# A rewritten order for ACT and DVE at the seam between the mixer and the feed-forward

## The chip, the cores and the metric

The kernel runs on one core of a Trainium2 chip. The metric is device time in microseconds (us), the median of several runs. PE is the matrix engine (TensorE), DVE the vector engine, ACT the scalar engine, POOL is GpSimd; SP issues most of the loads. A time inside the program is counted from the start of the profiled span.

## What is computed

One encoder layer on 512 rows of 1024 columns, in fp32:

```python
u = rms_norm(h, g_mix[i])
z = u @ w_in[i]
...                                     # two kinds of attention, each projected: y_a, y_b
mixed = gates[:, :, 0] * y_a + gates[:, :, 1] * y_b
h = h + mixed @ w_mix_out[i]            # the mixer's output
u = rms_norm(h, g_mlp[i])
h = h + jnp.square(jax.nn.relu(u @ w_ff1[i])) @ w_ff2[i]        # D_FF = 4096
ple_gate = jax.nn.sigmoid(rms_norm(h, g_ple[i]) @ w_ple_gate[i])
h = h + ple_gate * (p[i] @ w_ple_proj[i])
return rms_norm(h, g_final)
```

The change lies around the lines from the mixer's output to the feed-forward.

## The kernel before

**Split operands.** A product of fp32 matrices is made of three matmul passes over operands split in two: hi (a rounded copy) and lo (what is left), as hi·hi, hi·lo and lo·hi. The weights are split on the chip, in units of 128x1024 that are numbered in the order of use (u59h and u59l are the two parts of unit 59). ACT casts hi and DVE subtracts to get lo:

```python
nc.scalar.copy(hi[:, z], src[:, z])                                              # L329
nc.vector.tensor_tensor(lo[:, z], src[:, z], hi[:, z].bitcast(F32), ALU.subtract)  # L330
```

The hi and the lo parts have rings of four buffers each. `advance(i)` emits the splits up to unit i at the place in the program where it is called.

**Seven products for eight.** Blocks of 2x2 are multiplied by seven products, numbered 1, 2, 5, 6, 7, 3, 4 in the code. Products 5, 6, 7 and 4 take a weight that is a sum of quadrants, made in place in the loaded tile by `sum_source`: by a DVE add (L301) for the keys named there, else by a DMA from POOL's queue that adds into its target (L303). A sum for 6 may be made only when the unit of 5, whose tile it changes, is split.

**The feed-forward.** It runs in four quarters of 28 products each. A key ("f1", g, pn) is product pn with the first matrix for column group g, ("s2", g, pn) with the second. The list `steps` gives the order; quarter 1 in its short form, where a and b are ("f1", 0, .) and ("f1", 1, .), A and B ("s2", 0, .) and ("s2", 1, .):

```
a1 b1 a2 b2 a5 b5 a6 b6 a7 a3 b7 b3 A1 a4 b4 B1 A2 A5 B5 B2 A6 B6 A3 A7 B7 B3 A4 B4
```

These are units u59 to u86, so a1 is u59, a5 u63, a6 u65, A1 u71, B5 u77 and B6 u80; quarter 2 begins with u87. Before each product the loop over `steps` emits the evacuation of the one before (L925 copy, L929 add; into h_sb at L1122 and L1124), the activation (`ff1_act`: relu, square, cast; `ff1_lo`, L1430), the operands of the second matrix (`ff2_op`: L1415 to L1419, whose hi and lo are made at L72 and L73), the splits (`advance(last_unit(n + 2))`: two products ahead) and the weight sums.

**From the mixer to the quarter.** The mixer's last products end with h_sb = mxx + h_sb, and `part_ssq` (ACT, L1132) takes sums of squares of the rows. Each of the four row blocks then goes through: n_ms and n_rs on POOL (L364, L367: the factor of the norm), n_xn on DVE (L374), transposes n_tr on PE (L1192), and `put`, which writes hi (ACT, L1208) and lo (DVE, L1216) of the operands. For row blocks 2 and 3 the sums of operand quadrants s1 to s4 and their copies a21 are made on top of that (`t2_sums`, `t2_sums2`, `t2_sums34`, `t2_rest`). Independent of all that are eight products with w_ple_proj, pp 0 to 7 (L76 to L78, pspp, copied to ppo and spilled), which fill PE between the norms and transposes.

**What sets the order.** On PE and POOL it is always the order of the program. On ACT and DVE it is the order of the program from the mixer's output to step 3 of quarter 1 (`man.close()` at n == 3), and elsewhere a scheduler's. SP's order is the scheduler's. An engine takes its instructions strictly in order, so one that waits holds up all behind it.

Of the kernel before, what the change touches and what calls it, by code (L numbers as in the profile page):

```python
# [52 lines left out]
def layer_kernel(ctx: ExitStack, tc: tile.TileContext, x, p, g_mix, w_in, b_forget, swa_sinks,  # L53
# [32 lines left out]
    raws, order, unit_of = [], [], {}  # L86
# [77 lines left out]
    for t in MIX_STEPS.split():  # L164
# [3 lines left out]
        elif t[1:] in "04":  # L168
            half = int(t[1:]) // 4
# [9 lines left out]
            for j, u in enumerate(rows(w_ple_gate, r4 * 512, half * 512, f"wpg{half}{r4}")):  # L179
                add(("pg", half, 2 * r4 + j), u)  # L180

    look = {"split": 2, "dma": 4, "ahead": 3, "wp2": None, "n": 0, "d": 0}

    def raws_of(i):
        r, pn = order[i][1][:2]
# [95 lines left out]
    def sum_source(i):  # L281

        if i in sources or i >= len(order) or not isinstance(order[i][1][0], (list, dict)):
            return
        emit_dma(i)
        key, (rs, pn, _), _ = order[i]

        first = {5: 1, 6: 5, 4: 6}.get(pn)  # L290
        if (first and unit_of[key[:-1] + (first,)] >= look["n"]
                or pn == 7 and unit_of[key[:-1] + (5,)] not in sources
                or any(raws[r]["tile"] is None for r in raws_of(i))):
            return
        if pn in (1, 2, 3):
            q = quadrant(i, pn in (2, 3), pn == 3)
        else:
            q = quadrant(i, 0, pn == 7)
            other = quadrant(i, *{5: (0, 1), 7: (1, 1), 6: (1, 1), 4: (1, 0)}[pn])
            if key[0] == "s2" and pn in (5, 7) or key == ("f1", 1, 6):  # L300
                nc.vector.tensor_tensor(q, q, other, ALU.add)  # L301
            else:
                nc.gpsimd.dma_start(q, other, accum_op=ALU.add)  # L303
        sources[i] = q if key[0] != "f1" and key[0] != "g" else q.rearrange("q k (j c) -> q k j c", c=P)
# [28 lines left out]
    def advance(i):  # L333

        while look["n"] < min(len(order), i + 1):
            n = look["n"]
            emit_split(n)
            look["n"] += 1
            emit_dma(min(len(order) - 1, look["n"] + look["ahead"]))
            if isinstance(order[n][1][0], (list, dict)):  # L340

                key = order[n][0]
                for pn in {1: (5,), 5: (6, 7), 6: (4,)}.get(key[-1], ()):
                    if key[0] != "s2" or pn in (6, 4):
                        sum_source(unit_of[key[:-1] + (pn,)])

    def unit(key):
        i = unit_of[key]
# [834 lines left out]

    trs = {}

    def t2_pe(tb):
        for half in range(2):
            tr = trs[tb, half] = psA.tile([P, 4, P], F32, tag="tr", bufs=3,
                                          name=f"n2_{tb}_tr{half}")
            for j in range(4):  # L1190
                k = half * 4 + j
                nc.tensor.transpose(tr[:, j, :], xn2[tb][:, k * P:(k + 1) * P], ident)  # L1192
# [4 lines left out]
    def put(pn, tb, src, between=None):  # L1197
        sl = t2_cols(tb)
        k, parts = 0, []
        for hi, lo in zip(*u_op[pn]):  # L1200
            n = hi.shape[1]
            parts.append((hi[sl], lo[sl], src[:, k:k + n]))
            k += n
        for hi, lo, part in parts:
            if pn == 3:
                nc.scalar.mul(hi, part, -1.0)
            else:
                nc.scalar.copy(hi, part)  # L1208
# [22 lines left out]
        put(4, tb, trs[tb, 1],  # L1231
            lambda: nc.vector.tensor_tensor(s1, trs[tb, 1], a21, ALU.subtract))

    def t2_sums2(tb):
        a21, s1, s2, s3, s4 = sums[tb]
        nc.vector.scalar_tensor_tensor(s2, s1, -1.0, a_raw[0][t2_cols(tb)], ALU.mult,
                                       ALU.subtract)
        put(6, tb, s2)

    def t2_sums34(tb):  # L1240
        a21, s1, s2, s3, s4 = sums[tb]
        nc.vector.tensor_tensor(s3, a_raw[0][t2_cols(tb)], a21, ALU.subtract)
        nc.vector.tensor_tensor(s4, a_raw[1][t2_cols(tb)], s2, ALU.add)

    def t2_rest(pn):
        new_op(pn)
        for tb in (2, 3):
            put(pn, tb, sums[tb][{5: 1, 7: 3, 3: 4}[pn]])

    def scale2(tb):  # L1250
        rs = rms_rstd(acc2[tb], f"n2_{tb}")
        xn2[tb] = norm_scale(h_sb[:, tb, :], rs, gb, wk3, f"n2_{tb}")
# [56 lines left out]
    MIX_TAGS = {1: ("x", "sc"), 2: ("y", "tr"), 5: ("z", "mm"), 6: ("x", ""), 7: ("x", ""),  # L1309
                4: ("x", ""), 3: ("z", "")}  # L1310

    def mix_out(pn):
        for i in range(2):
            tb, half = rows_out("mx", MIX_TAGS, pn, i)
            if pn in (2, 3, 7, 4):
                part_ssq(acc2[tb], tb, half, "2")

    f1_0 = unit_of["f1", 0, 1]
# [2 lines left out]
    for t in MIX_STEPS.split():  # L1321
        if t == "B5":
            mix_ops(1, (3,))
            mxp.close()
            r_st.close()
            wk3 = ctx.enter_context(tc.tile_pool(name="wk3", bufs=2))
            look["place"] = ff_other
            p_sb = [tmp(f"p_sb{n}", (P, 2, 256)) for n in range(2)]
            for n in range(2):
                nc.sync.dma_start(p_sb[n], p[n * 256:n * 256 + 256, :]  # L1330
                                  .rearrange("(t q) c -> q t c", q=P))
            with nc.allow_non_contiguous_dma(reason="one word per partition and chunk"):
                nc.sync.dma_start(g_ple_t, g_ple[0].rearrange("(k q) -> q k", q=P))
        if done[:1] == "B":
            mix_out(int(done[1]))
        if t == "p4":
            break
        if t == "A5":
            mix_ops(1, (5,))
        if t == "B2":  # L1340
            mix_ops(1, (7, 6))
        if t == "B3":
            p_transposed()
        if t == "p0":
            scale2(0)
        key = ("mx", "AB".index(t[0]), int(t[1])) if t != "p0" else ("pp", 0)
        if t == "A4":
            scale2(1)
        if t == "B4":
            t2_pe(0)  # L1350
            new_u2()
            t2_top(0)
        advance(min(unit_of[key] + (4 if t in ("A1", "A2", "B1") else 3), f1_0))
        for n in range(look["n"], min(unit_of[key] + 5, f1_0)):
            sum_source(n)
        if t in ("A1", "A2"):
            mix_sum(1, 0 if t == "A1" else 2)
            mix_sum(1, 1 if t == "A1" else 3)
        if t == "p0":
            pp_put(0, pp_mm(0))  # L1360
        else:
            rows_mm("mx", t[0] == "A", MIX_TAGS, key, mix_op[key[1:]])
        done = t
# [84 lines left out]
    def last_unit(n):  # L1448
        return unit_of[steps[min(n, len(steps) - 1)]]


    look["split"] = 0
    t2_pe(1)
    ps = pp_mm(1)
    t2_top(1)
    scale2(2)
    scale2(3)
    pp_put(1, ps)
    pp_put(2, pp_mm(2))
    pp_put(3, pp_mm(3))  # L1460
    ps = pp_mm(4)
    t2_pe(2)
    t2_sums(2)
    pp_put(4, ps)
    advance(f1_0 + 1)
    t2_pe(3)
    t2_sums2(2)
    t2_sums(3)
    pp_put(5, pp_mm(5))
    advance(f1_0 + 2)  # L1470
    t2_sums2(3)
    pp_put(6, pp_mm(6))
    pp_put(7, pp_mm(7))
    advance(f1_0 + 3)
    t2_rest(5)
    done, late, later = None, None, {}
    for n, st_ in enumerate(steps):
        res = None
        if done is not None:
            if done[0] == "f1":  # L1480
                res = win_out(done[:2], done[2], tmp)
                if res is not None:
                    src, dst, i, e = res
                    res = src, dst, done[1], i, e
                if done[2] == 4:
                    for w, pn in ((1, 5), (1, 6), (5, 3), (6, 7)):
                        later.setdefault(n + w, []).append((done[1], pn))
            elif done[1] % 2:
                s2_out(done[1] // 2, done[2])
        if late is not None:  # L1490
            ff1_lo(*late)
        for g, pn in later.pop(n, ()):
            ff2_op(g, pn)
        if n > 0:
            advance(last_unit(n + 2))
            for i in range(look["n"], last_unit(n + 3) + 1):
                sum_source(i)
        if n in (3, 4):
            t2_sums34(n - 1)
        if n in (5, 6):  # L1500
            t2_rest({5: 7, 6: 3}[n])
        late = None if res is None else ff1_act(*res)
        if st_[0] == "f1":
            win_mm(st_[:2], st_[2], u_op[st_[2]], {})
        else:
            s2_mm(*st_[1:])
        if n == len(steps) - 2:
            t3(0)
        done = st_
        if n == 3:  # L1510
            man.close()
    s2_out(3, 4)
    t3(1)
# [112 lines left out]
```

## Time and profile before

| | |
|---|---|
| runs | 717.55, 717.98, 718.2 us |
| median | 717.98 us |
| profiled execution | 719.32 us |
| its span, first to last instruction | 717.6 us |
| granted TensorE clock | 0.997 |
| busy: PE, DVE, ACT, POOL | 702.9, 550.5, 456.6, 87.8 us |
| quarter 1, first matmul of u59 to that of u87 | 347.93 to 429.63: 81.70 us |
| quarter 2 | 429.63 to 506.04: 76.41 us |
| mean rate of the DMA | 168 GB/s |

The busy line gives each engine's share of the span. A window's row has the stretch, its length, and busy time with the number of instructions for each engine in it. A timeline row has start, duration, engine, line, operation, output and inputs without buffer numbers, and in brackets the idle time of the engine before it with what ended it. A row of PE's waits has the total, the number of times and the longest wait.

### The profile page before, as it was taken

To read this page: it belongs to the slowest core of one execution; us is meant where nothing else is said; L and a number is where in the kernel's file an instruction comes from. 1 tells how busy PE (TensorE), PEld (TensorE's weight loads), DVE (VectorE), ACT (ScalarE), POOL (GpSimd) and SP (SyncE) were. 2 spreads that over 40 slices of the span, in tenths; PEclk is the share of its full clock that TensorE was granted. 3 is DMA by queue.
4 is the path that set the end of the run, shared out by engine and by line. 5 is a ranking of instruction groups with operands and counts; after the bars stand their busy time and mean duration, and the time that the engine had idled before them with its cause. 6 is when DMAs were issued, how large, how long until landed. Compare 5 with 4: busy or idle time off the path is not lost.

```text
span 717.6 us, 11507 instructions
## 1 busy us (share of the span) xinstructions
PE 702.9 (98%) x4205; PEld 622.3 (87%) x4205; DVE 550.5 (77%) x941; ACT 456.6 (64%) x851; POOL 87.8 (12%) x129
## 2 busy tenths in 40 slices
PE   8999999999999999999999999999999999999996
PEld 7988888888888998888989779988998899988785
DVE  6557888877696766877799885899579965996565
ACT  5547888779862564347688536874487547865452
POOL 1011211100001200203020102010200020010101
PEclk9999999999999999999999999999999999999998
DMA  8256456670355796697597598749895689268003
GB/s 282 74 159 159 110 134 154 151 198 2 118 175 118 150 334 221 118 268 215 162 197 258 98 289 170 245 79 254 179 258 118 152 237 231 94 140 292 1 4 114
DMA packets 75432, 120.40 MB, mean 168 GB/s; under 512 B 6888, under 2 KB 44784, under 8 KB 75376
## 3 DMA queue, kind: packets, MB, share of 16 engines
q1 hardware_dynamic: 66016, 86.25, 37.9%
q0 software_dynamic: 9072, 33.03, 24.9%
q8 instruction: 33, 0.54, 0.3%
q10 hardware_dynamic: 288, 0.39, 0.2%
q14 instruction: 23, 0.19, 0.1%
HBM read 72.93 MB, written 4.19 MB: 107 GB/s over the span
## 4 chain that ended last, share of the span: by engine, by line
PE 64%; DVE 13%; DMA 9%; issue 8%; ACT 5%; SPq 1%; POOL 0%; POOLq 0%; ACTq 0%; DVEq 0%
DMA wq<-wq 5%; PE pf L76 5%; PE pf L78 5%; PE pf L77 5%; PE mxx L1300 3%; PE h_sc L765 3%; PE (1, 's2')x L1300 2%; PE h_pv L835 2%; PE h_tr L823 2%; PE psy L76 2%; PE psy L77 2%; PE psy L78 2%; PE vb L479 2%; PE va L479 2%; PE ('g', 1, 2)x L914 2%
## 5 line engine op out<-in xcount | busy, mean ns | idle before, releaser
L303 POOL DMA_DIRECT2D wq<-wq x36 | 31.3, 961 | 227.3 <-DVE u43l L330 30.4
L783 ACT ACTIVATE s<-s,h_nm 128x128 f32<-128x128 f32 (+1 forms) x64 | 32.6, 512 | 5.9 <-DVE h_nm L776 5.2
L73 DVE TENSOR_TENSOR h_ptl<-h_tr,h_pth 128x512 fp32r<-128x512 f32 (+2 forms) x40 | 22.9, 604 | 4.0 <-ACT h_pth L72 3.6
L72 ACT CAST h_pth<-h_tr 128x512 fp32r<-128x512 f32 (+2 forms) x40 | 19.4, 523 | 1.8 <-PE h_tr L823 1.4
L479 PE MATMUL va<-wv_h,u 128*128 128x320 f32 x64 | 20.1, 318 | 0.3 <-ACT u L72 0.3
L823 PE MATMUL h_tr<-ident,s 128*128 128x128 f32 x136 | 19.6, 277 | 0.2
L479 PE MATMUL vb<-wv_h,u 128*128 128x328 f32 x64 | 19.6, 313 | 0.0
L303 POOL DMA_DIRECT2D wgw<-wgw x8 | 7.1, 971 | 101.7 <-DVE u25l L330 77.7
L364 POOL TENSOR_SCALAR n_ms<-acc 128x1 f32<-128x1 f32 x15 | 5.6, 370 | 99.3 <-ACT sgp L1533 38.5
L1132 ACT ACTIVATE junk<-h_sb 128x512 f32<-128x512 f32 x16 | 10.0, 626 | 11.6 <-DVE h_sb L1124 7.0
L835 PE MATMUL h_pv<-h_ptl,v 128*128 128x256 f32 (+1 forms) x64 | 16.9, 305 | 0.4 <-DVE h_ptl L73 0.3
L835 PE MATMUL h_pv<-h_pth,v 128*128 128x256 f32 (+1 forms) x64 | 17.3, 290 | 0.0
L1528 DVE TENSOR_TENSOR sgp<-sgp,pp 128x512 f32<-128x512 f32 (+1 forms) x9 | 5.7, 633 | 14.5 <-ACT sgp L1527 14.5
L823 PEld LDWEIGHTS h_tr<-ident,s 128*128 128x128 f32 x136 | 15.0, 141 | 2.0 <-ACT s L803 0.5
L803 ACT ACTIVATE s<-s,h_rec 128x128 f32<-128x128 f32 (+2 forms) x32 | 14.2, 483 | 2.4 <-DVE h_rec L797 2.4
L845 DVE TENSOR_TENSOR h_ao<-h_pv,h_ao 64x512 f32<-64x512 f32 x16 | 10.9, 681 | 6.0 <-ACT h_ao L844 5.8
L771 DVE CUSTOM_DVE_ANT_0 s<-h_sc,causal 128x128 f32<-128x128 f32 (+3 forms) x32 | 13.8, 483 | 0.3 <-PE h_sc L765 0.3
L797 DVE RECIPROCAL h_rec<-h_den 128x4 f32<-128x4 f32 x16 | 3.0, 185 | 14.5 <-ACT s L783 14.3
L1527 ACT ACTIVATE sgp<-psgt,rs 128x512 f32<-128x512 f32 x7 | 4.8, 687 | 14.2 <-PE psgt L78 14.2
L835 PEld LDWEIGHTS h_pv<-h_ptl,v 128*128 128x128 f32 x64 | 12.1, 188 | 1.7 <-DVE h_ptl L73 0.8
L73 DVE TENSOR_TENSOR u<-n_tr,u 128x512 fp32r<-128x512 f32 x16 | 10.5, 684 | 3.9 <-ACT u L72 3.9
L771 DVE CUSTOM_DVE_ANT_0 s<-h_sc,bswa 128x256 f32<-128x256 f32 (+1 forms) x32 | 10.7, 384 | 3.1 <-PE h_sc L765 3.1
(1645 smaller groups left out, 2783.3 us busy)
## 6 DMA issues: line engine op xcount, KB each, us to landing
wq<-in_w_ff_dram SPq DMA_DIRECT2D x43, 512.0 KB, 6.3
wq<-wq POOLq DMA_DIRECT2D x36, 512.0 KB, 5.9
wq_c<-in_w_ff_dram SPq DMA_DIRECT2D x9, 512.0 KB, 6.3
wg<-in_w_in_dram SPq DMA_DIRECT2D x4, 1024.0 KB, 5.6
wgw<-in_w_in_dram SPq DMA_DIRECT2D x8, 512.0 KB, 4.8
wgw<-wgw POOLq DMA_DIRECT2D x8, 512.0 KB, 5.8
wq<-in_w_mix_out_dram SPq DMA_DIRECT2D x8, 512.0 KB, 5.4
wpg<-in_w_ple_gate_dram SPq DMA_DIRECT2D x4, 1024.0 KB, 8.7
```

The lines of the kernel that those rows point to most:

```text
L73: nc.vector.tensor_tensor(lo, src, hi.bitcast(F32), ALU.subtract)
L76: nc.tensor.matmul(ps, lh, rh, start=start, stop=False)
L77: nc.tensor.matmul(ps, lh, rl, start=False, stop=False)
L78: nc.tensor.matmul(ps, ll, rh, start=False, stop=stop)
L303: nc.gpsimd.dma_start(q, other, accum_op=ALU.add)
L479: nc.tensor.matmul(ps, u[:, kk_, ts_], w[:, kk_, c0:c1], start=kk_ == 0 and n == 0, stop=kk_ == KT - 1 and n == 2)
L765: nc.tensor.matmul(ps[:, off:off + n], qs[i][z][:, qb * P:(qb + 1) * P], kk[i][z][:, k0:k0 + n], start=z == 0, stop=z == 1)
L771: nc.vector.tensor_tensor_reduce(out=s[:, o:o + n], in0=ps[:, off:off + n], in1=c["bias"](qb), scale=1.0, scalar=NEG, op0=ALU.add, op1=ALU ...
L783: nc.scalar.activation(sl, sl, AF.Exp, bias=nm[:, qb:qb + 1], accum_out=den[:, qb:qb + 1])
L823: nc.tensor.transpose(tr[:, n, :], c["s"][:, o, :], ident)
L835: nc.tensor.matmul(pv[:, q0:q0 + nq, :], V2[kb][:, c["v"], :], t[:, o:o + nq, :], start=n == 0, stop=n == 2 * NT - 1, skip_group_check=True)
L1300: nc.tensor.matmul(bank[bkey, bk, i], o, w, start=tg != "" and n == 0, stop=n == 5, skip_group_check=True)
```

## The change

- The sum for ("f1", 0, 6), u65, is made by a DVE add; it was a POOL DMA. That for ("f1", 1, 6) was a DVE add already.
- u59 and u60 are split right after the mixer's last h_sb additions, before the sums of squares of row blocks 2 and 3. Their weight sums on POOL (for u63 and u64) are held in a list and issued after n_2_rs.
- The norm of row block 2 is emitted before the operands of row block 1; u61 is split after pp 3, u62 among the operands of row block 2. On PE the first half of row block 2's transposes stands before pp 4, the second half after it, and row block 3's after pp 5.
- s3 and s4 of both row blocks are computed before quarter 1 instead of at its steps 3 and 4, the operands for products 7 and 3 are written at steps 3 and 4 instead of 5 and 6.
- In steps 1 to 4 of quarter 1 splits are emitted three products ahead instead of two, and the hand-written order ends at step 5 instead of 3.

```diff
-            if key[0] == "s2" and pn in (5, 7) or key == ("f1", 1, 6):
+            if key[0] == "s2" and pn in (5, 7) or key in (("f1", 0, 6), ("f1", 1, 6)):
                 nc.vector.tensor_tensor(q, q, other, ALU.add)
             else:
                 nc.gpsimd.dma_start(q, other, accum_op=ALU.add)
...
-                    if key[0] != "s2" or pn in (6, 4):
+                    if key[0] == "s2" and pn not in (6, 4):
+                        continue
+                    if look["held"] is None:
                         sum_source(unit_of[key[:-1] + (pn,)])
+                    else:
+                        look["held"].append(unit_of[key[:-1] + (pn,)])
...
-    def mix_out(pn):
-        for i in range(2):
-            tb, half = rows_out("mx", MIX_TAGS, pn, i)
-            if pn in (2, 3, 7, 4):
+    def mix_out(pn, between=None):
+        done = [rows_out("mx", MIX_TAGS, pn, i) for i in range(2)]
+        if between is not None:
+            between()
+        if pn in (2, 3, 7, 4):
+            for tb, half in done:
                 part_ssq(acc2[tb], tb, half, "2")
...
     look["split"] = 0
+    look["held"] = []
+    mix_out(4, lambda: advance(f1_0 + 1))
     t2_pe(1)
-    ps = pp_mm(1)
+    scale2(2)
+    held, look["held"] = look["held"], None
+    for n in held:
+        sum_source(n)
     t2_top(1)
-    scale2(2)
     scale2(3)
-    pp_put(1, ps)
-    pp_put(2, pp_mm(2))
-    pp_put(3, pp_mm(3))
+    for n in (1, 2, 3):
+        pp_put(n, pp_mm(n))
+    advance(f1_0 + 2)
+    t2_pe(2, (0,))
     ps = pp_mm(4)
-    t2_pe(2)
+    t2_pe(2, (1,))
     t2_sums(2)
+    t2_sum2(2)
+    advance(f1_0 + 3)
     pp_put(4, ps)
-    advance(f1_0 + 1)
+    t2_rest(6, (2,))
+    ps = pp_mm(5)
     t2_pe(3)
-    t2_sums2(2)
     t2_sums(3)
-    pp_put(5, pp_mm(5))
-    advance(f1_0 + 2)
-    t2_sums2(3)
+    t2_sum2(3)
+    pp_put(5, ps)
+    t2_sums34(2)
+    t2_rest(6, (3,))
+    t2_rest(5)
+    t2_sums34(3)
     pp_put(6, pp_mm(6))
     pp_put(7, pp_mm(7))
-    advance(f1_0 + 3)
-    t2_rest(5)
...
         if n > 0:
-            advance(last_unit(n + 2))
+            advance(last_unit(n + (3 if n < 5 else 2)))
...
         if n in (3, 4):
-            t2_sums34(n - 1)
-        if n in (5, 6):
-            t2_rest({5: 7, 6: 3}[n])
+            t2_rest({3: 7, 4: 3}[n])
...
-        if n == 3:
+        if n == 5:
             man.close()
```

Three places in the order of the instructions. Lines of the new kernel have numbers 4 to 12 higher.

DVE at the end of the mixer, before, from the norm of row block 1 (n_1_xn) on; u_3822 is the operand that `put` writes:

```order
L374 SCALAR_TENSOR_TENSOR n_1_xn<-h_sb,n_1_rs,g_mlp_bc 128x512 x2
L330 TENSOR_TENSOR u59l<-wq_3414,u59h 128x1024
L1216 TENSOR_TENSOR u_3822<-n_0_tr_3812,u_3822 128x128
L1216 TENSOR_TENSOR u_3822<-n_0_tr_3812,u_3822 128x3x128
L1216 TENSOR_TENSOR u_3822<-n_0_tr_3817,u_3822 128x4x128
L1122 TENSOR_TENSOR h_sb<-mxx_3508,h_sb 128x512
L1122 TENSOR_TENSOR h_sb<-mxx_3515,h_sb 128x512
L1216 TENSOR_TENSOR u_3822<-n_1_tr_3850,u_3822 128x128
L1216 TENSOR_TENSOR u_3822<-n_1_tr_3850,u_3822 128x3x128
L1216 TENSOR_TENSOR u_3822<-n_1_tr_3855,u_3822 128x4x128
L374 SCALAR_TENSOR_TENSOR n_2_xn<-h_sb,n_2_rs,g_mlp_bc 128x512 x2
L374 SCALAR_TENSOR_TENSOR n_3_xn<-h_sb,n_3_rs,g_mlp_bc 128x512 x2
```

The same place now, from the last additions into h_sb on:

```order
L1126 TENSOR_TENSOR h_sb<-mxx_3508,h_sb 128x512
L1126 TENSOR_TENSOR h_sb<-mxx_3515,h_sb 128x512
L330 TENSOR_TENSOR u59l<-wq_3414,u59h 128x1024
L330 TENSOR_TENSOR u60l<-wq_3321,u60h 128x1024
L378 SCALAR_TENSOR_TENSOR n_2_xn<-h_sb,n_2_rs,g_mlp_bc 128x512 x2
L1220 TENSOR_TENSOR u_3817<-n_1_tr_3853,u_3817 128x128
L1220 TENSOR_TENSOR u_3817<-n_1_tr_3853,u_3817 128x3x128
L1220 TENSOR_TENSOR u_3817<-n_1_tr_3858,u_3817 128x4x128
L378 SCALAR_TENSOR_TENSOR n_3_xn<-h_sb,n_3_rs,g_mlp_bc 128x512 x2
L330 TENSOR_TENSOR u61l<-wq_3414,u61h 128x1024
```

u59l and u60l have moved between the last h_sb and n_2_xn, the operands of row block 1 behind n_2_xn, and u61l up to the norms.

POOL's queue before, from row block 2's norm on; the DMAs are the weight sums for u64 (wq_3321<-wq_3191), u65 (wq_3414<-wq_3258), u67 and u69; that for u63 stands ahead of these rows:

```order
L303 DMA wq_3414<-wq_3191 128x1024
L364 TENSOR_SCALAR n_2_ms<-acc_2_3498 128x1
L367 TENSOR_TENSOR n_2_rs<-n_2_ms,mhalf 128x1
L364 TENSOR_SCALAR n_3_ms<-acc_3_3499 128x1
L367 TENSOR_TENSOR n_3_rs<-n_3_ms,mhalf 128x1
L303 DMA wq_3321<-wq_3191 128x1024
L303 DMA wq_3414<-wq_3258 128x1024
L303 DMA wq_3191<-wq_3258 128x1024
L303 DMA wq_3191<-wq_3321 128x1024
```

And now:

```order
L368 TENSOR_SCALAR n_2_ms<-acc_2_3498 128x1
L371 TENSOR_TENSOR n_2_rs<-n_2_ms,mhalf 128x1
L303 DMA wq_3414<-wq_3191 128x1024
L303 DMA wq_3321<-wq_3191 128x1024
L368 TENSOR_SCALAR n_3_ms<-acc_3_3499 128x1
L371 TENSOR_TENSOR n_3_rs<-n_3_ms,mhalf 128x1
L303 DMA wq_3191<-wq_3258 128x1024
L303 DMA wq_3191<-wq_3321 128x1024
```

The sums for u63 and u64 now stand between the norms of row blocks 2 and 3, and the one for u65 is gone from the queue.

DVE between u76l and u77l, before; z, r and u are outputs of the first matrix's products and o operands of the second:

```order
L330 TENSOR_TENSOR u76l<-wq_3258,u76h 128x1024
L1415 TENSOR_TENSOR z_('f1', 0)_4178<-z_('f1', 0)_4178,r_4476 128x512
L301 TENSOR_TENSOR wq_3191<-wq_3191,wq_3321 128x1024
L1418 TENSOR_TENSOR r_4476<-u_('f1', 0)_4039,r_4476 128x512
L73 TENSOR_TENSOR o_0_5_4504<-z_('f1', 0)_4178,o_0_5_4504 128x512
L1419 SCALAR_TENSOR_TENSOR u_('f1', 0)_4039<-z_('f1', 0)_4178,u_('f1', 0)_4039 128x512
L1122 TENSOR_TENSOR h_sb<-(0, 's2')x_4428,h_sb 128x512
L1122 TENSOR_TENSOR h_sb<-(0, 's2')x_4435,h_sb 128x512
L1415 TENSOR_TENSOR z_('f1', 1)_4217<-z_('f1', 1)_4217,r_4476 128x512
L73 TENSOR_TENSOR o_06_4509<-u_('f1', 0)_4039,o_06_4509 128x512
L1418 TENSOR_TENSOR r_4476<-u_('f1', 1)_4066,r_4476 128x512
L73 TENSOR_TENSOR o_1_5_4535<-z_('f1', 1)_4217,o_1_5_4535 128x512
```

u77l comes two rows after these (one more L1419 stands between). Now:

```order
L301 TENSOR_TENSOR wq_3191<-wq_3191,wq_3321 128x1024
L330 TENSOR_TENSOR u76l<-wq_3258,u76h 128x1024
L1421 TENSOR_TENSOR z_('f1', 0)_4192<-z_('f1', 0)_4192,r_4476 128x512
L1424 TENSOR_TENSOR r_4476<-u_('f1', 0)_4043,r_4476 128x512
L330 TENSOR_TENSOR u77l<-wq_c_4114,u77h 128x1024
L73 TENSOR_TENSOR o_0_5_4504<-z_('f1', 0)_4192,o_0_5_4504 128x512
```

u77l has moved up in front of nine of the operations, with two left between it and u76l. Behind u82 the order of every engine is as before.

More of the change, by code (lines that the diff above doesn't have):

```diff
@@ L180, in layer_kernel @@
                 add(("pg", half, 2 * r4 + j), u)
-    look = {"split": 2, "dma": 4, "ahead": 3, "wp2": None, "n": 0, "d": 0}
+    look = {"held": None, "split": 2, "dma": 4, "ahead": 3, "wp2": None, "n": 0, "d": 0}
     def raws_of(i):
@@ L1184, in layer_kernel, with t2_pe @@
     trs = {}
-    def t2_pe(tb):
-        for half in range(2):
+    def t2_pe(tb, halves=(0, 1)):
+        for half in halves:
             tr = trs[tb, half] = psA.tile([P, 4, P], F32, tag="tr", bufs=3,
@@ L1232, in t2_sums, with t2_sum2 @@
             lambda: nc.vector.tensor_tensor(s1, trs[tb, 1], a21, ALU.subtract))
-    def t2_sums2(tb):
+    def t2_sum2(tb):
         a21, s1, s2, s3, s4 = sums[tb]
@@ L1237, in t2_sums2 @@
                                        ALU.subtract)
-        put(6, tb, s2)
     def t2_sums34(tb):
@@ L1243, in t2_sums34, with t2_rest @@
         nc.vector.tensor_tensor(s4, a_raw[1][t2_cols(tb)], s2, ALU.add)
[L1245 to L1248, printed above, removed]
+    def t2_rest(pn, tbs=(2, 3)):
+        if pn not in u_op:
+            new_op(pn)
+        for tb in tbs:
+            put(pn, tb, sums[tb][{5: 1, 6: 2, 7: 3, 3: 4}[pn]])
     def scale2(tb):
@@ L1333, in layer_kernel @@
                 nc.sync.dma_start(g_ple_t, g_ple[0].rearrange("(k q) -> q k", q=P))
+        if t == "p4":
+            break
         if done[:1] == "B":
             mix_out(int(done[1]))
-        if t == "p4":
-            break
         if t == "A5":
@@ L1352, in layer_kernel @@
             t2_top(0)
-        advance(min(unit_of[key] + (4 if t in ("A1", "A2", "B1") else 3), f1_0))
+        advance(min(unit_of[key] + (4 if t in ("A1", "A2", "B1") else 3), f1_0 - 1))
         for n in range(look["n"], min(unit_of[key] + 5, f1_0)):
```

## The prediction

> **What bounds the kernel now.** I read the page's busy line first, then busy time by stage, then what TensorE waited for, then the chain of waits.
>
> ```profile
> PE 702.9 (98%) x4205; PEld 622.3 (87%) x4205; DVE 550.5 (77%) x941; ACT 456.6 (64%) x851; POOL 87.8 (12%) x129
> ```
>
> PE at 98% looks like a bound that only fewer matmuls could move. The stages say otherwise. The four feed-forward quarters run the same 28 products each, so a quarter without stalls tells what another loses. The windows below are, in order: quarter 1 (first matmul of u59 to first of u87), quarters 2 and 3; a stretch of quarter 1 (u63 to u67) and its twin in quarter 2; a second stretch (u77 to u82) and its twin; the mixer's end; the middle of quarter 1.
>
> ```profile
> core 0: us, PE busy (x) PEld busy (x) DVE busy (x) ACT busy (x) POOL busy (x), PEclk, DMA share, GB/s
> 347.93:429.63 81.70, 78.72 (x505) 70.24 (x504) 72.97 (x91) 55.23 (x78) 9.50 (x11) 1.00 0.76 199
> 429.63:506.04 76.41, 76.41 (x506) 69.80 (x505) 63.43 (x75) 49.39 (x64) 10.40 (x12) 1.00 0.77 191
> 506.04:583.34 77.30, 77.08 (x506) 70.31 (x505) 63.44 (x75) 49.00 (x64) 10.40 (x12) 1.00 0.76 190
> 358.89:375.26 16.37, 15.06 (x122) 14.28 (x121) 15.51 (x20) 13.55 (x21) 4.35 (x5) 1.00 0.90 196
> 440.61:454.21 13.60, 13.60 (x123) 13.60 (x121) 8.11 (x8) 9.14 (x13) 1.70 (x2) 1.00 1.03 225
> 399.86:418.75 18.89, 17.22 (x73) 13.28 (x72) 16.77 (x22) 8.50 (x11) 2.57 (x3) 1.00 0.71 160
> 478.81:495.15 16.34, 16.34 (x73) 13.52 (x72) 16.34 (x23) 9.12 (x11) 1.72 (x2) 1.00 0.64 148
> 327.88:347.93 20.05, 20.05 (x106) 16.86 (x105) 16.23 (x27) 14.13 (x31) 3.56 (x6) 1.00 0.65 197
> 366.60:405.50 38.90, 38.24 (x260) 34.99 (x261) 38.74 (x49) 29.94 (x44) 4.27 (x5) 1.00 0.74 202
> ```
>
> Quarter 1 takes 81.70 us against 76.41 with 505 and 506 matmuls at the same clock: 5.29 us lost. The stretches place it: 16.37 − 13.60 = 2.77 at u63 to u67 and 18.89 − 16.34 = 2.55 at u77 to u82, together 5.32, so nothing is left elsewhere. At the mixer's end PE is busy for all of its 20.05 us. PE's waits in quarter 1:
>
> ```profile
> PE (0, 's2')z L1300 <- DVE u81l L330: 1.0, 1, 1.0
> PE ('f1', 0)x L914 <- DVE u65l L330: 0.8, 1, 0.8
> PE (0, 's2')z L1300 <- DVE u77l L330: 0.5, 1, 0.5
> PE ('f1', 0)x L914 <- ACT u65h L329: 0.4, 1, 0.4
> ```
>
> All four are splits that came too late; the rest of the 5.29 is matmuls stretched while they wait inside a product. The chain of waits (start us, us, what) shows why, first in stretch 1, then in stretch 2:
>
> ```profile
> 357.16 0.96 ACT u63h L329
> 358.14 1.24 DVE u63l L330
> 359.67 4.67 DMA wq<-wq
> ...
> 392.94 8.25 issue
> 401.20 5.16 DMA wq_c<-wq
> 406.38 1.06 ACT u80h L329
> 407.46 1.23 DVE u80l L330
> ...
> 411.69 1.14 DVE u81l L330
> ```
>
> **Stretch 1.** A split is an ACT cast and then a DVE subtract, and the next instruction in DVE's written order waits behind it. u63l ends at 359.38, when PE has reached that product (358.89). POOL's sum for u65 starts only then and takes 4.67 us to land, so u65h and u65l are late too.
>
> **Stretch 2.** DVE is busy for 38.74 of 38.90 us in the middle of the quarter, and its written order has twelve operations between u76l and u77l. u77l ends at 400.67; only then may POOL add into u80's source (5.16 us), and u80h, u80l and u81l follow in single file.
>
> **The change, part by part.**
>
> ```profile
> 359.67 2.64 POOL L303 DMA_DIRECT2D wq<-wq  x3 [12.00 <-DVE u63l L330]
> 361.62 1.21 DVE L301 TENSOR_TENSOR wq<-wq 128x1024 f32<-128x1024 f32 x1
> 341.80 1.41 DVE L374 SCALAR_TENSOR_TENSOR n_xn<-h_sb,n_rs,g_mlp_bc 128x512 f32<-128x512 f32 x2
> 343.21:358.14 14.93, 14.93 (x115) 14.11 (x114) 10.18 (x15) 10.72 (x21) 0.92 (x1) 1.00 0.50 143
> 390.56 1.22 DVE L330 TENSOR_TENSOR u76l<-wq,u76h 128x1024 fp32r<-128x1024 f32 x1
> 399.45 1.22 DVE L330 TENSOR_TENSOR u77l<-wq_c,u77h 128x1024 fp32r<-128x1024 f32 x1
> 390.56:412.83 22.27, 20.89 (x97) 16.82 (x95) 20.15 (x29) 13.76 (x19) 3.43 (x4) 1.00 0.50 92
> 335.79 1.28 DVE L1122 TENSOR_TENSOR h_sb<-mxx,h_sb 128x512 f32<-128x512 f32 x2
> 336.50 0.63 ACT L1132 ACTIVATE junk<-h_sb 128x512 f32<-128x512 f32 x1 [1.72 <-DVE h_sb L1122]
> 337.71 0.56 POOL L367 TENSOR_TENSOR n_rs<-n_ms,mhalf 128x1 f32<-128x1 f32 x1
> 340.48 2.73 DVE L374 SCALAR_TENSOR_TENSOR n_xn<-h_sb,n_rs,g_mlp_bc 128x512 f32<-128x512 f32 x4
> 340.63 0.39 PE L76 MATMUL pspp<-at_ff 128*128 128x512 f32 x1
> 341.99 1.99 PE L1192 MATMUL n_tr<-ident,n_xn 128*128 128x128 f32 x16
> 334.90 0.93 POOL L303 DMA_DIRECT2D wq<-wq  x1 [7.64 <-DVE u59l L330]
> ```
>
> 1. *The sum for ("f1",0,6) on DVE.* Gone is the first of three DMAs in POOL's queue (its 12.00 us wait and the other two queue behind it) and 4.67 us of transfer; added is one DVE add, 1.21 us by the row of ("f1",1,6), which is already made so. u65h then needs u63l plus 1.2 us, not u63l plus 4.7.
>
> 2. *Splits of u60 to u62 moved up.* From n_3_xn's end (341.80 + 1.41 = 343.21) to u63l's start at 358.14 DVE worked 10.18 us and idled 4.75, for casts that ACT's order had late. Now u60 is split before this stretch (−1.23), u61 and u62 stand before operands that wait for ACT, and s3 and s4 (four 128x512 operations; two queued take 1.28, so 0.6 each) fill in: 10.18 − 1.23 + 2.4 = 11.35. From n_3_xn's new end (342.5, point 3) u63l starts at 353.9 and ends at 355.1, without idle time; with all the old idle time at 359.9. ACT has one cast less there and its own order rewritten with DVE's, so I take 355, nearer the first. By then its source needs only its early POOL sum. Behind it stand two adds, u64l, one 0.6 and u65l: 355.1 + 2 × 1.21 + 1.23 + 0.6 + 1.23 = 360.6. PE wanted u65h at 365.52 less its 0.4 of waiting and less what u63 had cost by then, so at 364 or later. About 3.5 us are to spare in both places; the 2.77 goes unless three quarters of the idle time stay.
>
> 3. *u59 and u60 ahead of row block 2's norm.* DVE runs h_sb, u59l, u60l, n_2_xn: from 335.79 + 1.28 = 337.07 by 2 × 1.23 to 339.53, and the first half of n_2_xn (2.73 / 4 = 0.68) ends at 340.21. That grants nothing for u59l having left its old place ahead of h_sb. The first half of row block 2's transposes now follows pp3, not pp4, so PE wants it at 340.63: 0.42 us to spare at least. On ACT the two casts stand ahead of the sum of squares; ACT had idled 1.72 us there, and the casts need only weights that are loaded long before. I put n_2_rs at 338.4, ahead of u60l's end. Row block 3 has two POOL DMA issues (0.93 each) before its norm: 338.4 + 1.86 + n_ms and n_rs (two of 0.56 at most) = 341.4, n_3_xn to 342.5. PE comes to it after half a block of transposes (1.99 / 4 = 0.5), pp4 (341.99 − 340.63 = 1.36), 0.5 and pp5: 344.35. Cost: nothing while these two covers hold.
>
> 4. *Splits three products ahead, the hand order two products longer.* u77l now has two operations of 0.6 between it and u76l: with u76l no earlier than at 390.56 + 1.22 it ends at 394.1, 6.6 us sooner, and its 0.5 of waiting goes (PE comes there 2.77 sooner). u80's sum then lands about 6.6 us sooner too, and DVE's 2.12 idle (22.27 − 20.15) before u80l is gone: u81l ends at 412.83 − 2.12 = 410.7, less what DVE gains in stretch 1: 2.77 if it runs no further ahead of PE than before, 4.2 (359.38 − 355.1) at most. So 406.5 to 407.9. PE wanted it at 412.83 − 1.0, less 2.77 and about 1.3 of its own loss before it: 407.7. This is the thin place: 1.2 us to spare, or 0.2 short. I take it as met, since DVE is given idle time earlier that the old order did not have.
>
> 5. *DVE's total.* 72.97 + 1.21 − 1.23 (u60l) leaves 73 of 76.4 us, 95%: it fits, in a good order.
>
> 6. *DMA.* The loads that wait for s3 and s4 go out earlier; the order after u82 is unchanged, so quarters 2 to 4 move up one for one.
>
> The sum: 719.32 (profiled; span 717.6, 1.72 around it) − 5.29 = 714.03. The median of the runs is 717.98, 1.34 lower; from it, 712.69. Quarter 3, whose order has no such fault, still loses 77.30 − 76.41 = 0.89; between leftovers of 0 and 0.89 I take the middle, 0.45: **713.1 us**.
>
> [...]
>
> ```profile
> 325.62 1.23 DVE L330 TENSOR_TENSOR u56l<-wq,u56h 128x1024 fp32r<-128x1024 f32 x1 [1.75 <-ACT u56h L329]
> 325.67 1.60 POOL L367 TENSOR_TENSOR n_rs<-n_ms,mhalf 128x1 f32<-128x1 f32 x1
> ```
>
> This n_rs took 1.60 us where the one at 337.71 took 0.56, and it began 0.05 us after a subtract that reads two SBUF tiles. [...]
>
> **The rivals.**
> - *Only stretch 1 goes.* For it: DVE has no gap in 366.60 to 405.50, gets one more add, and u81l is thin by point 4. Then 717.98 − 2.77 = 715.2. Against it: u77l's new place.
> - *Given back.* At 95% DVE has no room for this order; stalls move to other splits, or the earlier loads and sums make one another late (the DMA share reaches 1.03 at 440.61). Within 1.4 us of before, about 717.5.
> - *Slower.* The chain h_sb, u59l, u60l, n_2_xn, transposes holds PE, which has a fixed order. Each microsecond beyond the 0.42 costs one. It cancels the gain when 4.84 + 0.42 = 5.3 us late, and shows as slower from 6.7 us on: 719.4. No row has such a delay; u59's or u60's piece would have to land that late.
>
> **How the numbers follow.** Two tenths of a per cent (1.44 us) is about what a measurement of this kernel can tell. Both stretches gone: 0.67, 712.3 to 714.3. Only the first: 0.21, 714.3 to 716. Given back: 0.07. Slower: 0.05. The range 712.3 to 715.6 leaves out the last two and the upper end of the second. Faster 0.88, same 0.07, slower 0.05.
>
> **What would show it.** Right: quarter 1 at 76.4 to 77.3 us; no wait of PE on u65l, u77l or u81l; PE full up to u59's first matmul at about 347.9; u63l ending near 355. Wrong: PE waiting for n_2_xn before u59; DVE without a gap from u69 to u80 and PE waiting on it; a u80h that still waits for its DMA.

## The result and the profile after

| | before | after |
|---|---|---|
| median, runs taken side by side | 717.76 us (716.24 to 718.2, 4 runs) | 711.05 us (710.52 to 711.52, 4 runs) |
| ratio after / before | | 0.991, 95% interval 0.9893 to 0.9927 |
| profiled execution, its span | 719.32, 717.6 us | 711.02, 709.3 us |

The changed kernel is faster by 6.7 us between the medians, and 711.05 lies under the low end of the predicted range, 712.3. Two more comparisons of the same two kernels gave 0.9919 (0.9905 to 0.9933) and 0.9928 (0.9915 to 0.9941), with 5.5 and 5.15 us between the medians.

The busy line of the changed kernel, and its time by stage in the prediction's order: quarters 1 and 2, stretch 1 (u63 to u67), stretch 2 (u77 to u82), the mixer's end up to the first matmul of u59.

```profile
PE 698.0 (98%) x4205; PEld 620.1 (87%) x4205; DVE 551.2 (78%) x942; ACT 457.2 (64%) x851; POOL 88.7 (13%) x128
```

```profile
core 0: us, PE busy (x) PEld busy (x) DVE busy (x) ACT busy (x) POOL busy (x), PEclk, DMA share, GB/s
347.17:424.18 77.01, 76.96 (x505) 69.80 (x504) 72.40 (x91) 53.65 (x76) 7.71 (x9) 1.00 0.78 210
424.18:500.58 76.40, 76.40 (x505) 69.80 (x504) 63.34 (x75) 49.38 (x64) 10.38 (x12) 1.00 0.77 193
358.14:372.03 13.89, 13.88 (x123) 13.69 (x121) 12.77 (x16) 12.46 (x20) 1.71 (x2) 1.00 0.79 207
396.63:413.30 16.67, 16.63 (x73) 13.44 (x72) 16.67 (x24) 9.02 (x11) 1.71 (x2) 1.00 0.64 161
327.12:347.17 20.05, 20.05 (x106) 16.70 (x104) 18.03 (x28) 15.86 (x33) 5.84 (x7) 1.00 0.67 175
```

The share of PE is 98% in both kernels and does not show the change; the stages do. Quarter 1 went from 81.70 to 77.01 us, stretch 1 from 16.37 to 13.89, stretch 2 from 18.89 to 16.67, and the mixer's end kept its 20.05. The view of PE's waits has no row at all for this quarter now. The splits that PE had waited for, and the add that now makes u65's weight sum (the second row), in the timeline of the changed kernel:

```profile
354.77 1.23 DVE L330 TENSOR_TENSOR u63l<-wq,u63h 128x1024 fp32r<-128x1024 f32 x1 [0.45 <-ACT u63h L329]
356.03 1.23 DVE L301 TENSOR_TENSOR wq<-wq,wq 128x1024 f32<-128x1024 f32 x1
360.17 1.22 DVE L330 TENSOR_TENSOR u65l<-wq,u65h 128x1024 fp32r<-128x1024 f32 x1
390.80 1.22 DVE L330 TENSOR_TENSOR u77l<-wq_c,u77h 128x1024 fp32r<-128x1024 f32 x1
406.16 1.22 DVE L330 TENSOR_TENSOR u81l<-wq,u81h 128x1024 fp32r<-128x1024 f32 x1
```

u63l ends at 356.00, 2.1 us before its product starts (358.14); u77l at 392.02, 4.6 us before (396.63). u81l ends 0.2 us before its product.

The stages of all kernels below, in us, from one profile each; "outside" is the span less quarter 1:

| kernel | u63 to u67 | u77 to u82 | quarter 1 | outside | ratio to before |
|---|---|---|---|---|---|
| before | 16.37 | 18.89 | 81.70 | 635.9 | |
| before, again | 16.44 | 18.64 | 81.87 | 633.0 | 1.000 (0.9988 to 1.0011) |
| before, third | 16.33 | 18.89 | 81.67 | 634.0 | 1.0006 (0.9995 to 1.0017) |
| after | 13.89 | 16.67 | 77.01 | 632.3 | 0.991 (0.9893 to 0.9927) |
| after, again | 13.89 | 16.34 | 76.69 | 632.4 | 0.9919 (0.9905 to 0.9933) |
| after, third | 13.99 | 16.35 | 77.10 | 632.1 | 0.9928 (0.9915 to 0.9941) |
| sum alone | 16.63 | 18.93 | 82.01 | 632.5 | 0.9994 (0.9985 to 1.0003) |
| three ahead alone | 21.72 | 16.35 | 84.51 | 633.9 | 1.0053 (1.0037 to 1.0069) |
| s3, s4 early alone | 16.63 | 16.40 | 81.47 | 634.3 | 1.0002 (0.9992 to 1.0011) |
| after, two ahead | 14.59 | 16.60 | 77.63 | 634.1 | 0.9941 (0.9926 to 0.9956) |
| after, u65's sum on POOL | 16.98 | 16.35 | 80.13 | 633.2 | 0.9978 (0.9969 to 0.9987) |
| the same, two ahead | 15.70 | 16.35 | 78.80 | 633.2 | 0.996 (0.9948 to 0.9972) |
| after, late splits | 16.72 | 18.33 | 81.50 | 633.0 | 0.9993 (0.9984 to 1.0003) |
| after, more sums on DVE | 14.00 | 16.35 | 77.10 | 633.7 | 0.9943 (0.9931 to 0.9955) |

### The profile page after: what moved, and what is told of

It is laid out like the page before. It is cut to its first block, busy times and chain, and to the rows that moved or that the text cites. A ratio compares the mean times of both kernels' runs of the same rounds, so it can differ in the third digit from the quotient of the medians.

```text
span 709.3 us, 11507 instructions
## 1 busy us (share of the span) xinstructions
PE 698.0 (98%) x4205; PEld 620.1 (87%) x4205; DVE 551.2 (78%) x942; ACT 457.2 (64%) x851; POOL 88.7 (13%) x128
## 4 chain that ended last, share of the span: by engine, by line
PE 89%; DVE 6%; issue 2%; DMA 2%; ACT 1%; POOL 0%; SPq 0%; POOLq 0%; DVEq 0%; ACTq 0%
PE pf L76 5%; PE pf L78 5%; PE pf L77 5%; PE (0, 's2')x L1304 3%; PE mxx L1304 3%; PE (2, 's2')x L1304 3%; PE (1, 's2')x L1304 3%; PE h_sc L769 3%; PE h_pv L839 2%; PE h_tr L827 2%; PE psy L76 2%; PE psy L78 2%; PE psy L77 2%; PE va L483 2%; PE vb L483 2%
```

## The experiments

**Both kernels again.** No edit. The question was where 6.7 us come from when quarter 1 gives 4.7.

> The kernel before, once more, for a second profile. The measured gain of the change (6.7 us between medians) is larger than the 4.7 us by which its first quarter became shorter; in the first pair of profiles quarters 3 and 4 of the old kernel also lost 0.9 and 0.7 us that the new one does not lose, and the time outside the four quarters differed by 2 us. Theory A (the rest is variation of the old kernel's transfers from one execution to the next): quarter 1 again takes 81.5 to 81.9 us, but quarters 3 and 4 lose another amount than 0.9 and 0.7, and the span differs by 1 us or more from 717.6. Theory B (the change also removes those later losses): 0.9 and 0.7 come back, within 0.2 each, and the ratio to the kernel before is 1.000.

> The changed kernel, once more, for a second profile and a better ratio. Theory A: quarter 1 takes 77.0 us again, the later quarters 76.4 plus 0 to 0.9, and the median gain over five rounds falls to 4.8 to 5.8 us (ratio 0.992 to 0.9935). Theory B: no loss in quarters 2 to 4, gain of 6.4 to 7 us again (ratio 0.990 to 0.991).

> The kernel before a third time, for the same: so far the span less quarter 1 was 635.9 and 633.0 us. Theory A: 632 to 635 us, a third value. Theory B: above 633.4 us, with losses again in quarter 3 or 4.

> The changed kernel a third time, for what lies outside quarter 1: so far the span less quarter 1 was 632.3 and 632.4 us. Theory A (variation of transfers): 632 to 634 us, losses of up to 0.9 us in the last quarters or behind them in some executions. Theory B (the change removes losses there): 632.0 to 632.6 again.

Quarter 1 is steady, at 81.67 to 81.87 us before and 76.69 to 77.10 after: on the means (81.75 and 76.93) the change is worth 4.8 us there. Quarter 3 of the old kernel is not steady. The same stage in its second and third profile:

```profile
505.62:582.04 76.42, 76.42 (x505) 69.73 (x504) 63.42 (x75) 49.26 (x64) 10.37 (x12) 1.00 0.77 192
```

```profile
505.49:581.89 76.40, 76.40 (x506) 69.80 (x504) 63.32 (x75) 49.29 (x64) 10.38 (x12) 1.00 0.78 194
```

So the 0.89 that the first profile lost in quarter 3 belonged to that execution, as theory A has it. The gain of 5.5 us in the second comparison fits theory A (4.8 to 5.8) and not theory B (6.4 to 7). The old kernel's runs in the three later comparisons had medians of 716.76 (23 runs), 717.14 (26) and 716.66 us (17). With 4.8 us from quarter 1, the gains of 6.7, 5.5 and 5.15 us between the two kernels' medians leave 1.9, 0.7 and 0.3 us for all that is outside it.

There the three profiles of the changed kernel lie at 632.1 to 632.4, those of the old one at 633.0 to 635.9 and the other kernels at 632.5 to 634.3. Behind u82 the order of DVE, ACT and POOL is the same in all of them, but for the kernel with more sums on DVE. The part that varies most is the end: from the first matmul of u170 on it takes 59.07, 57.86 and 59.35 us in the old kernel's profiles and 57.83, 57.29 and 57.82 in the changed kernel's, but 58.87 and 58.98 in two variants of the changed kernel (two ahead, more sums on DVE). So a long end is not bound to the old order. Whether the change makes it rarer stays open: the third pair of profiles (634.0 and 632.1) fits both theories, and theory B is not excluded.

**The weight sum on DVE alone.**

```diff
-            if key[0] == "s2" and pn in (5, 7) or key == ("f1", 1, 6):
+            if key[0] == "s2" and pn in (5, 7) or key in (("f1", 0, 6), ("f1", 1, 6)):
```

> The kernel before with only the weight sum of u65 on DVE in place of the POOL DMA. Theory: u63l still ends late (about 359.4), but u65's source is ready about 1.2 us after it in place of 4.7, so u65h no longer waits for a DMA; PE keeps the 0.5 us lost at u63 and loses little at u65 and u66: 2 us of stretch 1's 2.77 go, stretch 2 stays at 2.55 or gets up to 1.1 worse by the added DVE work. Quarter 1 about 79.7 to 80.8 us, ratio 0.997 to 0.999. Rival: the add stands in DVE's queue ahead of u64l and moves the lateness on to u64l and u65l, no gain: ratio 1.000 to 1.001.

The rival holds: no gain, with quarter 1 at 82.01 us in place of 79.7 to 80.8. The timeline shows the add made right behind u63l and u65h cast early. But seven operations stand between the add and u65l in DVE's order (three in the changed kernel):

```profile
358.51 1.23 DVE L301 TENSOR_TENSOR wq<-wq,wq 128x1024 f32<-128x1024 f32 x1
359.82 1.05 ACT L329 CAST u65h<-wq 128x1024 fp32r<-128x1024 f32 x1 [1.66 <-DVE wq L301]
364.92 1.22 DVE L330 TENSOR_TENSOR u65l<-wq,u65h 128x1024 fp32r<-128x1024 f32 x1
```

```profile
PE ('f1', 0)x L914 <- DVE u65l L330: 1.7, 1, 1.7
```

The 4.7 us of transfer are gone and u65h is cast at 359.82 where it was at 364.42. But u65l waits for its turn: PE's wait went from u65h (0.4) and u65l (0.8) to u65l alone (1.7).

**The changed kernel with the sum back on POOL**, the same line undone; and once more with splits two products ahead.

> The changed kernel with u65's weight sum on POOL again. In the changed kernel u63l ends 2.15 us before the product of u63 starts, and u65's product starts 5.44 us after that. A DMA issued behind u63l lands some 5.3 us later (issue and 4.7 us), so 3.2 us after u63's start; the cast and the subtract (1.05 and 1.23) end at 5.5 or later. Theory: PE loses 0 to 1 us at u65, quarter 1 at 76.8 to 78 us, so the add on DVE is worth under 1 us. Rival: the transfer is slowed beside the loads or queued behind other sums on POOL and costs 2 us or more at u65: quarter 1 above 78.7.

> The changed kernel with u65's sum on POOL and splits two products ahead: the seam's new order alone. With three ahead and the sum on POOL, ACT stood 5.1 us at the cast of u65h for that DMA, and the copies of finished products behind it were late (PE waited 1.8 us on one). Theory E (the loss is the queue behind the waiting cast): with two ahead more copies stand in front of that cast, so the wait on a copy shrinks and what is left is u65 itself, whose DMA lands some 5.3 us after u63l: stretch 1 at 14.3 to 16 us, below the 17.0 with three ahead. Rival F (the transfer is late for u65 by as much in any order): 16.5 us or more.

Against 0 to 1 us expected, undoing the one line costs 3.1 us of stretch 1 (16.98 against 13.89). The rival's time came (quarter 1 at 80.13), but PE does not lose it at u65. The timeline and PE's waits of the first:

```profile
361.32 1.05 ACT L329 CAST u65h<-wq 128x1024 fp32r<-128x1024 f32 x1 [5.14 <-DMA wq<-wq]
371.57 0.59 ACT L929 COPY u_('f1', 0)_4253<-('f1', 0)x 128x512 f32<-128x512 f32 x1
```

```profile
PE ('f1', 0)x L918 <- ACT u_('f1', 0)_4253 L929: 1.8, 1, 1.8
PE ('f1', 1)x L918 <- DVE u66l L330: 0.8, 1, 0.8
```

ACT stands idle for 5.14 us at u65h, with the copies of finished products queued behind it, and PE waits 1.8 us for one of those copies. u65l itself is just in time: it ends at 363.63, and PE comes to it at 363.60. With two ahead the wait on a copy is gone and stretch 1 is 15.70, in the range of theory E; PE then waits 0.8 us on u66l and 0.2 on u66h. The changed kernel with two ahead (below) takes 14.59. So the one line is worth 3.1 us with splits three products ahead and 1.1 with two, and the 2.0 between them is mostly the 1.8 us wait on the copy behind the waiting cast.

**The changed kernel with late splits.** u59 to u62 are split where the old kernel has them, and with them t2_rest(5) and row block 3's s3 and s4 come behind pp 6 and 7; the rest is as changed:

```diff
-    mix_out(4, lambda: advance(f1_0 + 1))
+    mix_out(4)
...
-        advance(min(unit_of[key] + (4 if t in ("A1", "A2", "B1") else 3), f1_0 - 1))
+        advance(min(unit_of[key] + (4 if t in ("A1", "A2", "B1") else 3), f1_0))
...
-    advance(f1_0 + 2)
     t2_pe(2, (0,))
...
     t2_sums(2)
+    advance(f1_0 + 1)
     t2_sum2(2)
-    advance(f1_0 + 3)
...
     t2_sums(3)
+    advance(f1_0 + 2)
     t2_sum2(3)
...
+    pp_put(6, pp_mm(6))
+    pp_put(7, pp_mm(7))
+    advance(f1_0 + 3)
     t2_rest(5)
     t2_sums34(3)
-    pp_put(6, pp_mm(6))
-    pp_put(7, pp_mm(7))
```

> The changed kernel with u59 to u62 split where the old kernel splits them (u59 before the last additions into h_sb, u60 to u62 among the operands), all else changed; u77l comes eleven operations behind u76l again. Theory: u63l is late again and stretch 1 is at 15 to 16.5 us (13.9 in the changed kernel), stretch 2 at 18.5 to 19 for u77l's place; quarter 1 at 80.5 to 82 us, near the old kernel. Rival: the add on DVE and the earlier s3 and s4 made stretch 1's gain, not the early splits: stretch 1 under 14.5 us.

As the theory has it, quarter 1 is at 81.50 us and nearly all of the gain is gone, though both stretches lie just outside what was expected (16.72 and 18.33). u63l ends at 358.71, when PE has been at its product since 358.01. In the changed kernel the early splits and the add need each other: stretch 1 is 16.98 without the add, 16.72 without the early splits and 13.89 with both, and the add alone in the old kernel gives 16.63. That neither is worth anything by itself is not shown: without the add, but with splits two ahead, stretch 1 is 15.70, 0.7 under the old kernel. What row block 2's earlier norm and transposes and the held weight sums are worth by themselves no run shows.

**Three ahead alone, and s3 and s4 early alone,** each put into the old kernel.

```diff
-            advance(last_unit(n + 2))
+            advance(last_unit(n + (3 if n < 5 else 2)))
...
-        if n == 3:
+        if n == 5:
             man.close()
```

```diff
     t2_rest(5)
+    t2_sums34(2)
+    t2_sums34(3)
...
         if n in (3, 4):
-            t2_sums34(n - 1)
-        if n in (5, 6):
-            t2_rest({5: 7, 6: 3}[n])
+            t2_rest({3: 7, 4: 3}[n])
```

> The kernel before with one thing of the change: splits three products ahead in steps 1 to 4 and the hand order to step 5. Its DVE order has u77l two operations behind u76l, as in the changed kernel, though u77 is split long after the hand order ends. Theory C: stretch 2 (u77 to u82, 18.9 us before, 16.3 without loss) hangs on u77l's place in the order alone: 16.3 to 16.8 us here, while stretch 1 (u63 to u67, 16.4 before, 13.6 without loss) still has its late u63l and stays at 15.5 to 16.5; quarter 1 at 79 to 79.6 us, ratio about 0.9965. Rival D: stretch 2 needs the lead that DVE gains in stretch 1; then it stays above 17.5 us and quarter 1 above 80.5.

> The kernel before with another thing of the change alone: s3 and s4 of row blocks 2 and 3 made ahead of quarter 1, their operands for products 7 and 3 at steps 3 and 4. Here, too, u77l stands two operations behind u76l. Theory C: stretch 2 is 16.3 to 16.8 us; stretch 1 has 2.4 us more DVE work ahead of u63l, which fills idle time for the most part, and less behind it: 15 to 17.5 us. Quarter 1 at 78.7 to 81 us. Rival D: stretch 2 above 17.5 us.

Both miss the time that was expected, since they make what lies ahead of stretch 2 worse, and yet both clear stretch 2. Its windows in the two profiles:

```profile
404.56:420.91 16.35, 16.35 (x73) 13.52 (x72) 16.35 (x23) 9.12 (x11) 1.71 (x2) 1.00 0.65 152
```

```profile
401.48:417.88 16.40, 16.40 (x74) 13.44 (x72) 16.40 (x23) 9.06 (x11) 1.71 (x2) 1.00 0.62 147
```

Theory C holds for stretch 2 and D falls: no lead from stretch 1 is needed. In both, as in all kernels of the table whose stretch 2 takes 16.3 to 16.7 us, two operations stand between u76l and u77l on DVE; in the kernels with eleven or twelve there (before, the sum alone, late splits) it takes 18.3 to 18.9 us. u77 is the nineteenth product of the quarter, long behind the end of the hand order, so the scheduler chooses its place, and either of these two changes ahead of it is enough to make it choose the other one. No run has three ahead without the longer hand order.

Three ahead alone makes the kernel 0.5% slower: stretch 1 takes 21.72 us where 15.5 to 16.5 were expected. ACT waits at u65h, and PE for a copy behind it, as above:

```profile
362.74 1.06 ACT L329 CAST u65h<-wq 128x1024 fp32r<-128x1024 f32 x1 [4.86 <-DMA wq<-wq]
PE ('f1', 0)x L914 <- ACT u_('f1', 0)_4253 L925: 4.0, 1, 4.0
```

With s3 and s4 early alone, quarter 1 is at 81.47 us in place of 78.7 to 81. The added work stands ahead of u63l, and here PE waits for u63h before stretch 1 begins: from u59 to u63 it takes 12.96 us, against 10.96 or 10.97 in the other kernels.

```profile
PE ('f1', 0)z L914 <- ACT u63h L329: 1.8, 1, 1.8
```

**The changed kernel with splits two products ahead.**

```diff
-            advance(last_unit(n + (3 if n < 5 else 2)))
+            advance(last_unit(n + 2))
```

> The changed kernel with splits emitted two products ahead in quarter 1, as before the change (the rest of the change stays, with the hand order to step 5). Theory: stretch 1 stays without loss, since its splits hang on the rewritten order ahead of the quarter; of stretch 2's 2.55 us at least half comes back, since u77l stands behind its twelve operations again: quarter 1 at 78.3 to 79.6 us, 1.3 to 2.6 us over the changed kernel. Rival: the lead that DVE gains in stretch 1 carries stretch 2 alone, and the time is that of the changed kernel within 0.5 us.

The expectation was wrong in its place: u77l keeps its place two operations behind u76l, stretch 2 stays at 16.60 us, and the third product ahead is worth 0.7 us in stretch 1 (14.59 against 13.89), where PE waits 0.5 us on u65l. The median is 712.72 us (711.79 to 714.68) against 711.24 for the changed kernel in the same comparison.

**More sums on DVE.** The sums of product 6 for the first column group of quarters 2 to 4:

```diff
-            if key[0] == "s2" and pn in (5, 7) or key in (("f1", 0, 6), ("f1", 1, 6)):
+            if key[0] == "s2" and pn in (5, 7) or key[0] == "f1" and pn == 6 and (key[1] < 2 or key[1] % 2 == 0):
```

> The changed kernel with the weight sums of product 6 for the first column group made on DVE in quarters 2 to 4 also, three adds of 1.2 us in place of three POOL DMAs. The old kernel's quarters 3 and 4 lost 0 to 0.9 us, differently in each profile, where the sums of a quarter's head queue behind late loads. Theory: one transfer less in that burst brings the others in 1 to 2 us sooner, quarters 2 and 3 take 76.4 us and the stretch u143 to u170 74.5 us in every execution; 0 to 0.5 us faster than the changed kernel, with nothing lost on DVE, which idles 13 us per later quarter. Rival: the add waits at the head of DVE's queue for its source and holds up the subtracts behind it: a quarter above 77 us, slower than the changed kernel by 0.5 us or more.

No gain: quarter 3 takes 76.40 us, as in the changed kernel's profiles, so there was nothing to remove, and the median is 712.54 us (711.91 to 714.04) against 711.51 (710.5 to 712.22). The rival's sign, a quarter above 77 us, did not come either in quarters 2 and 3. In the profile the difference lies at the end (58.98 us from u170 on, 57.3 to 57.8 in the changed kernel's three profiles). As two ahead has 58.87 there without these adds, the cause stays open.

## Why the prediction was wrong in its number

In quarter 1 the mechanism was right, and with the leftover counted there the time came out where the sum had put it: 81.70 − 5.29 + 0.45 = 76.86, measured 77.01, 76.69 and 77.10. Two other terms of the sum failed: its base, which was too high, and the gain outside quarter 1, which it put at nothing.

- **The base (failed).** The sum went out from 717.98, the median of three runs. The old kernel's later medians, over 23, 26 and 17 runs, are 716.76, 717.14 and 716.66, so the term was 0.8 to 1.3 us too high. Of these 66 runs 17 took 717.55 us, the lowest of the three, or more, and the fourth run beside the three took 716.24; why the three were all high stays open. From 716.7 the same sum gives 711.9 us. The range began 0.4 us under the sum without a leftover and had no room for such an error; begun 1.3 us lower, it would have 711.05 at its very edge.
- **Quarters 2 to 4 and the end (failed).** Point 6 has all behind u82 "move up one for one", and the sum had no term for a gain there. The medians differ by 6.7, 5.5 and 5.15 us where 4.84 was forecast and quarter 1 gives 4.8: 1.9, 0.7 and 0.3 us come from outside it. The old kernel's first profile had lost 0.89 in quarter 3, which did not come back, and had a long end (59.07 us from u170 on), which came back in one of two further profiles. Since the order there is unchanged and variants of the changed kernel show a long end too, part of this is variation between executions; whether all of it is stays open.
- **The leftover.** That its size was right (0.3 to 0.7 us in quarter 1) is luck. It was taken from quarter 3's 0.89, which was no property of the order, and what is left in quarter 1 is something else: in all three profiles u66 and u67 take 2.84 to 2.93 us where a product of quarter 2 takes 2.72, without a wait in the view; why stays open.
- **Point 1, the sum.** Right in the full change, and an essential part. That u65h "needs u63l plus 1.2 us" held: u63l ended at 356.00 and the add at 357.26. That this helps depended on the early splits and, by the timeline of the sum alone, on u65l's new place.
- **Point 2, the early splits.** Right in kind. u63l ended 8.8 us after the first matmul of u59, not 7.2 as worked out. Most of this is n_3_xn, which ended at 343.31, 3.9 us ahead of that matmul, in place of 5.4 (342.5 to 347.93): n_2_rs was held up (point 3), and n_3_xn takes 1.42 us where the working left 1.1. Another 0.45 is idle time ahead of u63l. So 2.1 us were to spare in place of 3.5.
- **Point 3, the mixer's end.** Right: it cost nothing. The cover was thinner than 0.42 us, since the norm of row block 2 was held up on POOL. The timeline of the changed kernel:

```profile
335.85 1.22 DVE L330 TENSOR_TENSOR u59l<-wq,u59h 128x1024 fp32r<-128x1024 f32 x1
336.61 1.68 POOL L368 TENSOR_SCALAR n_ms<-acc 128x1 f32<-128x1 f32 x1 [10.11 <-ACT junk L1136]
336.98 1.22 DVE L330 TENSOR_TENSOR u60l<-wq,u60h 128x1024 fp32r<-128x1024 f32 x1
338.37 0.56 POOL L371 TENSOR_TENSOR n_rs<-n_ms,mhalf 128x1 f32<-128x1 f32 x1
338.96 1.41 DVE L378 SCALAR_TENSOR_TENSOR n_xn<-h_sb,n_rs,g_mlp_bc 128x512 f32<-128x512 f32 x2 [0.76 <-POOL n_rs L371]
339.63 0.39 PE L78 MATMUL pspp<-at_ff 128*128 128x512 f32 x1
339.86 0.63 PE L1196 MATMUL n_tr<-ident,n_xn 128*128 128x128 f32 x4
```

  n_ms, which takes 0.30 us for row block 3, took 1.68 here: it began during u59l and ended at 338.29, 0.09 us after u60l (338.20). In the kernel with late splits, where neither subtract runs beside it, the same n_ms takes 0.29, as it does in the old kernel (at 337.33):

```profile
336.44 0.29 POOL L368 TENSOR_SCALAR n_ms<-acc 128x1 f32<-128x1 f32 x1 [1.50 <-ACT junk L1136]
```

  The 1.68 us are like the 1.60 us of the n_rs beside u56l in the old kernel. That the subtracts held n_ms up is the author's reading of these lengths; how they would do it, no run shows. n_ms, which came during u59l, did not end with it (337.07) but behind u60l. So the delay, 1.68 − 0.30 = 1.38 us, fell on n_2_ms, and n_2_rs took 0.56, as at 337.71 in the old kernel. DVE lost 0.76 us to it; the first half of n_xn (about 0.70) ended near 339.66 and PE came to it at 339.86, so 0.2 us of cover was left and PE lost nothing.
- **Point 4, stretch 2.** The gain was right (2.2 to 2.5 us of 2.55), the reason half wrong. u77l's place decides, and that the prediction had; but the third product ahead is only one way to that place (s3 and s4 early, or the rest of the change without it, give the same), and the lead out of stretch 1 is not needed. The thin place was real: u81l had 0.2 us to spare, and stretch 2 took 16.67 us in one profile and 16.34 and 16.35 in the others.
- **Point 5, DVE's total.** 72.40 us measured, 73 forecast; it fits.
- **The rivals.** None came: PE has no wait on u77l or u81l, quarter 2 took 76.40 us, and row block 2's transposes were in time.

## What to carry to other kernels

Three runs did not fix the base of this forecast to better than 1 us: the range needs the spread of the base beside that of the change. A loss that one profile shows in one of several equal stages may belong to that execution alone. A late operand can have two causes in series (a transfer, then a place in a written order), and here taking away one moved the wait to the other (PE's 0.4 us on u65h and 0.8 on u65l became 1.7 on u65l): test the parts singly and together. Emitting work further ahead can cost more than it gains while its source is late: here a cast that waited 4.86 us stood in front of the copies of PE's outputs, and PE waited 4.0 us for one of them.

## What the runs showed of the hardware

The 4.0 us wait in the kernel with three ahead alone cost more than its length. Three stretches of its windows view, ahead of, in and behind the wait's end:

```profile
371.00:373.00 2.00, 0.55 (x5) 0.35 (x4) 2.00 (x4) 2.00 (x5) 0.00 (x0) 1.00 1.13 197
373.00:376.00 3.00, 0.49 (x4) 0.49 (x5) 3.00 (x5) 2.95 (x6) 0.00 (x0) 0.99 0.91 307
376.00:380.00 4.00, 4.00 (x24) 4.00 (x23) 1.47 (x2) 0.00 (x0) 0.00 (x0) 0.58 1.03 352
```

PE stood from 371.56 to 375.51, and then the granted clock was 0.58 on the mean from 376 to 380: by an estimate from these numbers the matmuls of that stretch took about 1.7 us longer (4.0 × 0.42). The product of u67, 375.51 to 379.96, took 4.45 us where a product of quarter 2 takes 2.72. Why the clock fell there is not shown: it is one wait in one profile. The 1.8 us wait in the kernel with the sum on POOL left the clock at 1.00 (358.16 to 375.14).
